# An encoder layer on one core: row scale applied after the projection, head norms ahead of weights, and decayed HGRN keys on GpSimd

## The chip, the cores and the metric

The kernel runs on one core of one Trainium2 chip. The metric is the device time of one execution in microseconds; the median of three runs stands for the kernel. One of the executions is profiled, and all durations below come from that one. Engines are called by the profile's names: PE (TensorE), DVE (VectorE), ACT (ScalarE), POOL (GpSimd) and SP (SyncE, which issues most transfers).

## The reference, cut to what matters

```python
xn = rmsnorm(h, norm_mix[l])            # h: 16 meta tokens and 256 tokens, 2048 wide
proj = xn @ w_in[l]                     # 2048 x 5120
q, f_logit, i_in, g_out, u = jnp.split(proj, [D_HG, 2 * D_HG, 3 * D_HG, 4 * D_HG], axis=-1)
o_hg = hgrn2_mixer(q, f_logit, i_in, g_out, lb_all[l], hg_norm[l])   # 8 heads, 128x128 state
o_s5 = s5_mixer(u, ...)                 # 64 groups, diagonal complex scan, GELU, GLU
h = h + jnp.concatenate([o_hg, o_s5], -1) @ w_out[l]
h = h + conv_ffn(rmsnorm(h, norm_ffn[l]), w_ffn_gate[l], w_ffn_up[l], ..., w_ffn_down[l])
return rmsnorm(h[:, N_META:], final_norm)

def rmsnorm(x, g):                      # one scale per token, one gain per channel
    return x * lax.rsqrt(jnp.mean(x * x, axis=-1, keepdims=True) + EPS) * g
```

## The kernel before, in words

Everything lives in SBUF with channels on the 128 partitions and the 272 tokens along the free dimension. A float32 product is made of three float32r products on PE (`mm3`, lines 193 to 195): high part times high part, high weights times low activations, low weights times high activations. So every operand is split into a high part (a cast on ACT) and a low part (a subtraction). `wload` brings 1 MB of weights into `raw`, `wsplit` makes `whi` on ACT (line 169) and `wlo` on DVE (recorded under the helper `tt`, line 92). There are three buffers of `raw` and three halves of `whi` and `wlo`.

The program begins with a head (lines 220 to 347). It loads x in four pieces, forms for each token the sum of squares and from it the row scale (`row_rs`, `sqrt_rs`), spreads the row scales of the 272 tokens over all partitions with small matmuls into `rbs`, transposes x into `xT`, and for each of 16 channel blocks makes `xn = xT * gm * rbs` on DVE (line 339; `gm` is the gain column times -0.5, which undoes a factor that the row scale carries), `xh` on ACT (line 340) and `xl` on DVE (line 341). The weights of the first chunk are split in quarters, six of the eight `wlo` on POOL. Ten small matmuls (line 312) run on PE ahead of the first product.

Then come 20 chunks of the input projection in the order of `ORDER`: u0, h0, u1, h1, and so on to g3. A `u` is one chunk of S5 channels, an `h` three chunks for two HGRN heads (f, q, i), a `g` one chunk of output gates. One chunk is 96 matmuls of 272 or 258 columns into two PSUM banks. Between the chunk matmuls PE runs the small float32 matmuls of the mixers. `s5_tile` projects (`bu`), scans on DVE with one addition on POOL (`m`, line 605) and projects back (`yps`). `hg_group` forms the scores of two heads level by level: blocks of 4 tokens first (`dps`, with one reciprocal of the running products `SP` over all 512 columns, line 726), then for half lengths 4, 8, 16, 32 and 64 the decayed queries `qh` and keys `kt` (DVE, lines 738 and 740), a matmul `lps` on them, a masked copy into `S`, and `widen`, which multiplies the running products in `SP` and `f` (tile name `PP`) in place. `hg_cross` joins the two token blocks and writes `oT`.

After the chunks, `w_glu` (four units) works on the S5 output, and after unit 1 the head norm `hr` (from `hps` by three Newton steps on DVE) is spread per head by the matmuls `bps`, and `oT`, multiplied by gate and norm, is split into `mh` and `ml`. These are the operands of `w_out`. Then follow the gated MLP and the final norm, which are not touched.

The order of each engine's queue is fixed when the program is built: a scheduler takes the instruction with the lowest priority number that its own estimate says is ready. `pri(x)` shifts that number. Each engine runs its queue in order, and an instruction that waits holds up everything behind it.

Of the kernel before, what the change touches and what calls it, by code (L numbers as in the profile page):

```python
# [80 lines left out]
def hymba_kernel(ctx: ExitStack, tc: tile.TileContext, x, meta, lb_logits, norm_mix, w_in, hg_norm,  # L81
# [76 lines left out]
    def wsplit(raw, eng=(dve, dve), parts=1, dep=None):  # L158
        res = []
        n = 1024 // parts  # L160
        for hf in range(2):
# [2 lines left out]
            if dep is not None and dep[hf] is not None:

                act.copy(out=hi[:, 0:1], in_=dep[hf])
            for i in range(parts):
                c = slice(i * n, (i + 1) * n)
                act.copy(out=hi[:, c], in_=raw[:, hf, c])  # L169
                tt(lo[:, c], raw[:, hf, c], hi[:, c].bitcast(F32), SUB, eng[max(hf, i)])  # L170
# [129 lines left out]
    rm = row_rs(xm, NM, 1, "rm")  # L300
    rb = [None, None]
    for b in range(2):
        rb[b] = row_rs(xt[b], 128, 2, f"rb{b}")
        if b == 0:
            spread(rm, NM, rbp[0][:, 0:NM])
            spread(rb[0], 128, rbp[0][:, NM:])
            act.copy(out=rbs[:, 0:NM + 128], in_=rbp[0])
        else:
            spread(rb[1], 128, rbp[1][:, 0:128])
            dve.tensor_copy(out=rbs[:, NM + 128:T], in_=rbp[1][:, 0:128])  # L310
            for _ in range(NWARM2):
                pe.matmul(wps, ident, rbs[:, NM + 128:T], start=True, stop=True)
# [10 lines left out]
        if b == 0:  # L323
# [4 lines left out]
            gm = prm.tile([128, KD], F32, name="gm")  # L328
            gps = ptp.tile([128, KD], F32, tag="tp", name="gps")
            pe.transpose(gps, nrow, ident[0:KD, 0:KD])  # L330
            ts(gm, gps, -0.5, MUL)
# [468 lines left out]
    def do_u(c):  # L800
# [6 lines left out]
        if c == 1:  # L807
            c_kinds(1)
# [319 lines left out]
```

## Time and profile before

| what | value |
|---|---|
| median of 3 runs | 1227.13 us (1224.62 to 1233.77) |
| the profiled execution | 1229.55 us, its span 1227.8 us |
| PE busy | 1205.0 us, 98% of the span |
| DVE busy | 892.9 us, 73% |
| ACT busy | 623.6 us, 51% |
| POOL busy | 83.2 us, 7% |
| granted TensorE clock, mean | 0.993 |

The span is the time from the first to the last instruction of that execution; 1.75 us lie around it. A share is an average over stages: the 20 chunks end near 355 us, and from there to the end the engines other than PE have much less to do. Matmuls overlap, so that PE counts as busy from the start of one to the modelled end of the next; how far it is from its peak is seen from the distance between starts.

### The profile page before, as it was taken

Reading aid. Unit: us, or ns where it says so; the run is one execution under the profiler, and the core shown is the slowest. Engines: PE = TensorE matmul, PEld = TensorE weight load, DVE = VectorE, ACT = ScalarE, POOL = GpSimd, SP = SyncE. Lnnn points to the kernel's source line nnn. Section 1 sums busy time; section 2 is a strip of 40 time slices with the busy share of each in tenths; the row PEclk is TensorE's granted clock in tenths of the full one; section 3 lists DMA queues with packets and bytes.
Section 4 is the critical chain, followed back from the end, with each engine's and each line's share of the span. In section 5 each row is a group of like instructions: output and inputs, shape, how many; then the busy total and the mean of one; then the engine's idle time right before and its main releaser. Section 6 shows DMA issues by size and latency. Waiting matters only on the chain.

```text
span 1227.8 us, 21177 instructions
## 1 busy us (share of the span) xinstructions
PE 1205.0 (98%) x8531; PEld 1108.1 (90%) x8531; DVE 892.9 (73%) x1516; ACT 623.6 (51%) x1066; POOL 83.2 (7%) x102
## 2 busy tenths in 40 slices
PE   7989999999999999999999999999999999999997
PEld 6989999999989999999999999999999788888885
DVE  8988999999979778766666666765766555555554
ACT  6756667675655466444444444444443344444444
POOL 5231222111100000000000000000000000000000
PEclk9999999999999999999999999999999999999998
DMA  8544344434445555555655556565555545555552
GB/s 255 153 127 143 116 139 128 127 109 138 146 135 175 185 185 172 189 189 177 198 174 190 188 180 194 175 195 182 181 196 172 206 172 204 179 199 199 181 213 93
DMA packets 176289, 210.66 MB, mean 172 GB/s; under 512 B 14772, under 2 KB 168879, under 8 KB 170415
## 3 DMA queue, kind: packets, MB, share of 16 engines
q1 hardware_dynamic: 175871, 209.22, 52.4%
q8 instruction: 67, 1.10, 0.4%
q14 instruction: 31, 0.25, 0.1%
q0 software_dynamic: 320, 0.09, 0.0%
HBM read 206.08 MB, written 2.10 MB: 170 GB/s over the span
## 4 chain that ended last, share of the span: by engine, by line
PE 95%; DVE 2%; issue 1%; DMA 1%; ACT 1%; SPq 0%; POOL 0%; DVEq 0%; ACTq 0%; POOLq 0%
PE ua L976 13%; PE acc L193 10%; PE acc L194 9%; PE acc L195 9%; PE ga L193 7%; PE ga L195 7%; PE ga L194 7%; PE ua L982 7%; PE d L1047 7%; PE d L1049 7%; PE d L1048 7%; PE bu L623 1%; PE lps L753 1%; DVE xn L101 1%; DMA x<-in_x 0%
## 5 line engine op out<-in xcount | busy, mean ns | idle before, releaser
L92 DVE TENSOR_TENSOR wlo<-raw,whi 128x1024 fp32r<-128x1024 f32 (+1 forms) x376 | 462.0, 1229 | 288.6 <-ACT whi L169 238.7
L169 ACT CAST whi<-raw 128x1024 fp32r<-128x1024 f32 (+1 forms) x382 | 397.7, 1042 | 483.1 <-PE ga L194 157.4
L193 PE MATMUL ga<-fh,whi 128*128 128x258 f32 x704 | 198.9, 283 | 0.0
L195 PE MATMUL ga<-fh,wlo 128*128 128x258 f32 x704 | 198.1, 282 | 0.0
L194 PE MATMUL ga<-fl,whi 128*128 128x258 f32 x704 | 198.1, 282 | 0.0
L193 PE MATMUL acc<-xh,whi 128*128 128x272 f32 (+1 forms) x640 | 185.0, 293 | 3.1 <-ACT whi L169 3.1
L194 PE MATMUL acc<-xl,whi 128*128 128x272 f32 (+1 forms) x640 | 185.3, 291 | 1.9 <-DVE xl L92 1.9
L195 PE MATMUL acc<-xh,wlo 128*128 128x272 f32 (+1 forms) x640 | 183.2, 292 | 0.0
L194 PEld LDWEIGHTS ga<-fl,whi 128*128 128x128 f32 x704 | 133.6, 190 | 0.0
L193 PEld LDWEIGHTS ga<-fh,whi 128*128 128x128 f32 x704 | 133.1, 189 | 0.0
L195 PEld LDWEIGHTS ga<-fh,wlo 128*128 128x128 f32 x704 | 132.5, 189 | 0.0
L1048 PE MATMUL d<-whi,al 128*128 128x512 f32 x328 | 128.1, 391 | 0.0
L1047 PE MATMUL d<-whi,ah 128*128 128x512 f32 x328 | 127.4, 393 | 0.3 <-ACT ah L1040 0.3
L193 PEld LDWEIGHTS acc<-xh,whi 128*128 128x128 f32 x640 | 120.1, 189 | 7.1 <-ACT whi L169 3.3
L194 PEld LDWEIGHTS acc<-xl,whi 128*128 128x128 f32 x640 | 120.8, 189 | 4.7 <-DVE xl L92 2.8
L195 PEld LDWEIGHTS acc<-xh,wlo 128*128 128x128 f32 x640 | 119.6, 189 | 2.4 <-issue 1.0
L1049 PE MATMUL d<-wlo,ah 128*128 128x512 f32 x328 | 114.4, 390 | 0.0
L976 PE MATMUL ua<-fcxh,whi 128*128 128x512 f32 x352 | 96.6, 395 | 0.0
L976 PE MATMUL ua<-fcxl,whi 128*128 128x512 f32 x352 | 96.1, 394 | 0.0
L1047 PEld LDWEIGHTS d<-whi,ah 128*128 128x128 f32 x328 | 61.9, 189 | 13.3 <-ACT ah L1040 0.5
L1048 PEld LDWEIGHTS d<-whi,al 128*128 128x128 f32 x328 | 62.0, 189 | 12.9
L1049 PEld LDWEIGHTS d<-wlo,ah 128*128 128x128 f32 x328 | 61.9, 189 | 13.0
(417 smaller groups left out, 1897.7 us busy)
## 6 DMA issues: line engine op xcount, KB each, us to landing
raw<-in_w_ffn_gate SPq DMA_DIRECT2D x44, 1024.0 KB, 5.1
raw<-in_w_ffn_up SPq DMA_DIRECT2D x44, 1024.0 KB, 5.1
raw<-in_w_ffn_down SPq DMA_DIRECT2D x44, 1024.0 KB, 4.8
raw<-in_w_in SPq DMA_DIRECT2D x39, 1024.0 KB, 5.1
raw<-in_w_out SPq DMA_DIRECT2D x16, 1024.0 KB, 5.4
raw<-in_w_glu SPq DMA_DIRECT2D x4, 1024.0 KB, 4.9
x<-in_x SPq DMA_DIRECT2D x4, 512.0 KB, 5.6
out<-ob SPq DMA_DIRECT2D x8, 256.0 KB, 2.9
```

The costliest lines, as they stand in the source:

```text
L92: eng.tensor_tensor(out=dst, in0=a, in1=b, op=op)
L101: dve.scalar_tensor_tensor(out=dst, in0=a, scalar=s, in1=b, op0=op0, op1=op1, **kw)
L169: act.copy(out=hi[:, c], in_=raw[:, hf, c])
L193: pe.matmul(accs[m], lh, xh[:, n0:n1], start=first, stop=False)
L194: pe.matmul(accs[m], lh, xl[:, n0:n1], start=False, stop=False)
L195: pe.matmul(accs[m], ll, xh[:, n0:n1], start=False, stop=end)
L623: return pe.matmul(bus[i][:, ri], bt[h, 2 * ri + q0 // 2], R[h, q0 // 2], start=True, stop=True)
L976: pe.matmul(accs[m].rearrange("p a n -> p (a n)"), hi[:, k * 256 + m * 128:k * 256 + m * 128 + 128], c.rearrange("p a n -> p (a n)"), star ...
L982: pe.matmul(accs[m][:, 0], lo[:, k * 256 + m * 128:k * 256 + m * 128 + 128], c[:, 0], start=False, stop=(kt == KD - 1), skip_group_check=True)
L1047: pe.matmul(dps[t][n], ah[:, tk], hi, start=False, stop=False, skip_group_check=True)
L1048: pe.matmul(dps[t][n], al[:, tk], hi, start=False, stop=False, skip_group_check=True)
L1049: pe.matmul(dps[t][n], ah[:, tk], lo, start=False, stop=end, skip_group_check=True)
```

## The change

It takes the row scale out of the head. `xh` and `xl` are now the split of `xT * gm`, made by an ACT activation with a per-partition scale and one DVE operation, and `xn` and the ten small matmuls are gone. The row scales go to `rcol` (one column per token block) and, spread by three matmuls behind the first chunk, to `rbs`. Every consumer of a projection multiplies by them: `s5_u`, `hg_f`, `hg_q` and `hg_g` with a DVE `tt` from PSUM, `hg_i` by the scale of ACT copies that were there. The eight quarter splits of the first chunk's weights are chained on ACT by `issue_after`, and all eight `wlo` are on DVE. The S5 sum is written into the first half of `P`, whose layout is turned, and the tile `m` goes. The block of 4 tokens takes one reciprocal of 128 columns and builds the other three columns by products. The five larger keys go to POOL. `c_kinds(1)` moves behind the evacuation of u2, and the head norm chain gets `pri(-3)` inside its `pri(-2)`.

```diff
     def wunit(src):
         with pri(-4):
-            return wsplit(early.pop(0), (dve, pool), 2, deps.pop(0)) if early else wsplit(wload(src))
+            return units.pop(0) if units else wsplit(wload(src))
...
-    rm = row_rs(xm, NM, 1, "rm")
-    rb = [None, None]
+    gm = prm.tile([128, KD], F32, name="gm")
+    gps = ptp.tile([128, KD], F32, tag="tp", name="gps")
+    pe.transpose(gps, nrow, ident[0:KD, 0:KD])
+    dve.tensor_copy(out=gm, in_=gps)
...
-            for _ in range(NWARM2):
-                pe.matmul(wps, ident, rbs[:, NM + 128:T], start=True, stop=True)
...
+        def split():
+            i = act.copy(out=hi[:, c], in_=raw)
+            tt(lo[:, c], raw, hi[:, c].bitcast(F32), SUB)
+            return i.ins
+
+        if last is None:
+            wi = split()
+        else:
+            with tc.issue_after(last):
+                wi = split()
+        with tc.issue_after(wi):
+            for kt in (2 * p, 2 * p + 1):
+                last = act.activation(out=xh[:, kt], in_=xT[:, kt], func=AF.Identity, scale=gm[:, kt:kt + 1]).ins
+                stt(xl[:, kt], xT[:, kt], gm[:, kt:kt + 1], xh[:, kt].bitcast(F32), MUL, SUB)
+
+    rcol = s5p.tile([128, 3], F32, name="rcol")
+    rb = [row_rs(xt[0], 128, 2, "rb0")]
+    with pri(0.5):
+        rb += [row_rs(xt[1], 128, 2, "rb1"), row_rs(xm, NM, 1, "rm")]
+    for i, n in enumerate((128, 128, NM)):
+        ts(rcol[:n, i:i + 1], rb[i], -0.5, MUL)
...
-    for kt in range(KD):
-        xn = xin.tile([128, T], F32, tag="xn", name="xn", bufs=4)
-        stt(xn, xT[:, kt], gm[:, kt:kt + 1], rbs, MUL, MUL)
-        act.copy(out=xh[:, kt, :], in_=xn)
-        tt(xl[:, kt, :], xn, xh[:, kt, :].bitcast(F32), SUB)
...
-        act.copy(out=ysb[:, j], in_=pv)
+        tt(ysb[:, j], pv, rv, MUL)
...
-        m = s5w.tile([128, 2, 2 * TH], F32, tag="m", name="m", bufs=1)
-        tt(m, P[:, :, 0], P[:, :, 1], ADD, pool)
+        m = P[:, 0]
+        tt(m, m, P[:, 1], ADD, pool)
...
         for m in range(2):
+            tt(f[:, m], accs[m], rbs, MUL)
+        fact(k, f, AF.Sigmoid, scale=-1.0)
+        fact(f, f, AF.Sigmoid)
...
-            fact(sg[:, m], accs[m], AF.Sigmoid)
-            stt(q[:, m], accs[m], lbc[:, 1, h0 + m:h0 + m + 1], sg[:, m], MUL, MUL)
+            tt(q[:, m], accs[m], rbs[:, T0:T], MUL)
+        fact(sg, q, AF.Sigmoid)
+        for m in range(2):
+            stt(q[:, m], q[:, m], lbc[:, 1, h0 + m:h0 + m + 1], sg[:, m], MUL, MUL)
...
+        tt(r4[:, :, :, 0], s4[:, :, :, 0], f4[:, :, :, 3], MUL)
+        dve.reciprocal(out=r4[:, :, :, 0], in_=r4[:, :, :, 0])
+        tt(r4[:, :, :, 1], r4[:, :, :, 0], s4[:, :, :, 0], MUL)
+        tt(r4[:, :, :, 2], r4[:, :, :, 1], f4[:, :, :, 2], MUL)
+        tt(r4[:, :, :, 0:3], r4[:, :, :, 0:3], q4[:, :, :, 0:3], MUL)
+        act.copy(out=r4[:, :, :, 3], in_=q4[:, :, :, 3])
         widen(2)
         kt = kts[0]
-        dve.reciprocal(out=rv, in_=SP[:, :, NM:T])
         tt(kt.rearrange("p (m b) t -> p m (b t)", b=2), k[:, :, NM:T], SP[:, :, NM:T], MUL)
-        tt(qt, q[:, :, 2:NQ], rv, MUL)
...
             tt(halves(kt.rearrange("p (m b) t -> p m (b t)", b=2), h)[:, :, :, 0],
-               halves(k, h)[:, :, :, 0], halves(SP, h)[:, :, :, 0], MUL)
+               halves(k, h)[:, :, :, 0], halves(SP, h)[:, :, :, 0], MUL, pool)
...
+        if c == 0:
+            rbp = pmm.tile([128, T], F32, tag="mm", name="rbp")
+            spread(rcol[0:NM, 2:3], NM, rbp[:, 0:NM])
+            for b in range(2):
+                spread(rcol[:, b:b + 1], 128, rbp[:, NM + 128 * b:NM + 128 * (b + 1)])
+            act.copy(out=rbs, in_=rbp)
...
-        hrs = rsqrt(hgp, hps, [128, NQ], 1.0 / 128, "rh", tags=("iv", "qm", "v"))
+        with pri(-3):
+            hrs = rsqrt(hgp, hps, [128, NQ], 1.0 / 128, "rh", tags=("iv", "qm", "v"))
```

The change moves instructions on every engine. Three places matter below. The first is DVE in the head, from the last pieces of x to the first operands of the first chunk (`junk` is the discarded square, `rb1`, `rm` the row scales of the second token block and of the meta tokens). Before:

```order
L92 TENSOR_TENSOR wlo<-raw,whi 128x512
L101 SCALAR_TENSOR_TENSOR rb1y<-rb1t,rb1y 128x1
L322 COPY xT<-xps 128x4x128 x2
L310 COPY rbs<-rbp_155 128x128
L96 TENSOR_SCALAR gm<-gps 128x16
L101 SCALAR_TENSOR_TENSOR xn<-xT,gm,rbs 128x272 x4
L92 TENSOR_TENSOR xl<-xn,xh 128x272 x3
```

With the change:

```order
L100 SCALAR_TENSOR_TENSOR junk_139,rb1ss<-x_107 128x512
L95 TENSOR_SCALAR rcol<-rb0y 128x1
L305 COPY xT<-xps 128x4x128
L100 SCALAR_TENSOR_TENSOR junk_139,rmss<-xm 16x1024
L275 TENSOR_REDUCE rb1st<-rb1ss 128x1
L305 COPY xT<-xps 128x4x128
L275 TENSOR_REDUCE rmst<-rmss 16x1
L97 TENSOR_SCALAR rb1v<-rb1st 128x1
L91 TENSOR_TENSOR wlo<-raw,whi 128x512
L97 TENSOR_SCALAR rmv<-rmst 16x1
L100 SCALAR_TENSOR_TENSOR xl<-xT,gm,xh 128x272 x2
```

The first `xl` no longer stands behind the spreading of the row scales and four `xn`, but the square of the meta tokens now stands between the two last `xT` copies.

The second place is DVE in the levels of the first HGRN group, where `qh` is the decayed query and the two `widen` products are those on `SP` and `PP`; what an instruction waits for is in brackets:

```order
L91 TENSOR_TENSOR qh<-q,PP 128x256 [waits DVE_49]
L91 TENSOR_TENSOR SP<-SP,PP 128x34x8 [waits Pool_49]
L100 SCALAR_TENSOR_TENSOR pt<-pw 128x32 [waits DVE_49]
L100 SCALAR_TENSOR_TENSOR pw<-pw 128x32
L100 SCALAR_TENSOR_TENSOR W<-W,pw,tmp 128x2x34 [waits Activation_49] x2
L91 TENSOR_TENSOR PP<-PP 128x34x8 [waits DVE_49]
L91 TENSOR_TENSOR km<-k,SP 128x2x16
L95 TENSOR_SCALAR pw<-pt 128x32 [waits DVE_49]
L91 TENSOR_TENSOR wlo<-raw,whi 128x1024 [waits PE_49,Activation_49]
L91 TENSOR_TENSOR qh<-q,PP 128x256 [waits DVE_49]
```

The key that stood next to each `qh` has left DVE, and the in-place product on `SP` now waits until POOL has read `SP` for its key.

The third place is PE where `w_glu` ends and `w_out` begins. Before, the first spread of the head norm stands inside the third and fourth unit of `w_glu` (`gh` are the S5 operands):

```order
L194 MATMUL acc<-gh_4662,whi 128x258
L893 MATMUL bps<-hr,hsel 128x258 x2
L195 MATMUL acc<-gh_4662,wlo 128x258
L193 MATMUL acc<-gh_4663,whi 128x258
L194 MATMUL acc<-gh_4663,whi 128x258
```

With the change it stands behind the last one, right ahead of the first products that need `mh`:

```order
L188 MATMUL acc<-gh_4632,wlo 128x258
L918 MATMUL bps<-hr,hsel 128x258 x4
L186 MATMUL acc<-mh,whi 128x258 x3
L918 MATMUL bps<-hr,hsel 128x258 x2
L187 MATMUL acc<-ml,whi 128x258
L188 MATMUL acc<-mh,wlo 128x258
```

The first four `bps` have moved from between products of `w_glu` to the seam between the two matrices.

More of the change, by code (lines that the diff above doesn't have):

```diff
@@ L163, in wsplit @@
             lo = wsp.tile([128, 1024], F32R, tag="wlo", name="wlo")
[L164 to L170, printed above, removed]
+            act.copy(out=hi, in_=raw[:, hf])
+            tt(lo, raw[:, hf], hi.bitcast(F32), SUB)
             res.append((hi, lo))
@@ L234, in hymba_kernel @@
     sp.dma_start(out=xm, in_=meta)
+    sp.dma_start(out=nrow, in_=norm_mix.rearrange("o (r c) -> (o r) c", c=128))
     HD = D // 2
@@ L292, in hymba_kernel @@
         pe.matmul(wps, ident, ident, start=True, stop=True)
-    rbp = [pmm.tile([128, NM + 128], F32, tag="mm", name=f"rbp{b}") for b in range(2)]
-    rbs = xin.tile([128, T], F32, name="rbs")
+    rbs = s5p.tile([128, T], F32, name="rbs")
     def spread(r, n, ps):
         pe.matmul(ps, r.to_broadcast([n, 128]), ident[0:n, 0:n], start=True, stop=True)
-    rm = row_rs(xm, NM, 1, "rm")
-    rb = [None, None]
+    gm = prm.tile([128, KD], F32, name="gm")
+    gps = ptp.tile([128, KD], F32, tag="tp", name="gps")
+    pe.transpose(gps, nrow, ident[0:KD, 0:KD])
+    dve.tensor_copy(out=gm, in_=gps)
     for b in range(2):
[L303 to L310, printed above, removed]
-            for _ in range(NWARM2):
-                pe.matmul(wps, ident, rbs[:, NM + 128:T], start=True, stop=True)
         for i in range(4):
@@ L327, in hymba_kernel @@
             act.copy(out=xT[:, :, 0:NM], in_=xps)
[L328 to L331, printed above, removed]
+    last = None
+    for p in range(8):
+        u, hf, c = p // 4, p // 2 % 2, slice(512 * (p % 2), 512 * (p % 2) + 512)
+        if p % 4 == 0:
+            units.append([])
+        if p % 2 == 0:
+            units[u].append([wsp.tile([128, 1024], F32R, tag=t, name=t) for t in ("whi", "wlo")])
+        hi, lo = units[u][hf]
+        raw = early[u][:, hf, c]
+        def split():
[17 more added lines that the diff above has]
+        ts(rcol[:n, i:i + 1], rb[i], -0.5, MUL)
     tc.cur_priority += 900000
     pool.memset(ones, 1.0)
-    tc.cur_priority -= 900000
-    for kt in range(KD):
-        xn = xin.tile([128, T], F32, tag="xn", name="xn", bufs=4)
-        stt(xn, xT[:, kt], gm[:, kt:kt + 1], rbs, MUL, MUL)
-        act.copy(out=xh[:, kt, :], in_=xn)
-        tt(xl[:, kt, :], xn, xh[:, kt, :].bitcast(F32), SUB)
-    tc.cur_priority += 900000
-    deps[:] = [(None, xh[:, 0, 0:1].bitcast(F32)), tuple(xh[:, i, 0:1].bitcast(F32) for i in (3, 6))]
     vps = ptp.tile([128, 100], F32, tag="tp", name="vps")
@@ L568, in s5_u @@
     def s5_u(j, ps):
-        pv = ps.rearrange("p (k s) -> p s k", s=2)
-        act.copy(out=ysb[:, j], in_=pv)
+        pv, rv = (a.rearrange("p (k s) -> p s k", s=2) for a in (ps, rbs))
+        tt(ysb[:, j], pv, rv, MUL)
     def s5_split(j):
@@ L801, in do_u @@
         accs = chunk(w_in, 16 + c)
+        if c == 0:
+            rbp = pmm.tile([128, T], F32, tag="mm", name="rbp")
+            spread(rcol[0:NM, 2:3], NM, rbp[:, 0:NM])
+            for b in range(2):
+                spread(rcol[:, b:b + 1], 128, rbp[:, NM + 128 * b:NM + 128 * (b + 1)])
+            act.copy(out=rbs, in_=rbp)
         with pri(-3):
@@ L804, in do_u @@
                 s5_u(2 * c + m, accs[m])
+        if c == 2:
+            c_kinds(1)
         for m in range(2):
             s5_tile(2 * c + m, *s5_split(2 * c + m), *s5_b(2 * c + m))
[L807 to L808 removed]
     def do_h(g):
```

41 lines of the change are left out of this document (20 added, 21 removed).

## The prediction

> **What bounds the kernel now.** I read the busy shares first (busy us, share of the span, instructions of each engine).
>
> ```profile
> PE 1205.0 (98%) x8531; PEld 1108.1 (90%) x8531; DVE 892.9 (73%) x1516; ACT 623.6 (51%) x1066; POOL 83.2 (7%) x102
> ```
>
> PE sets the end, but the shares average over stages, so the table of stretches comes next (us; busy time and instructions of PE, PEld, DVE, ACT and POOL; granted clock; DMA share; GB/s).
>
> ```profile
> 17.00:20.40 3.40, 3.40 (x19) 3.40 (x19) 3.40 (x7) 2.78 (x8) 1.58 (x2) 0.54 1.13 332
> 20.00:100.00 80.00, 73.35 (x591) 70.66 (x591) 72.03 (x202) 49.39 (x101) 25.82 (x34) 0.98 0.51 150
> 85.20:88.60 3.40, 3.40 (x18) 3.40 (x18) 3.40 (x6) 0.87 (x2) 2.91 (x4) 0.53 1.03 340
> 100.00:300.00 200.00, 199.98 (x1789) 186.38 (x1789) 197.35 (x349) 133.41 (x331) 37.03 (x41) 1.00 0.41 126
> 300.00:355.00 55.00, 55.00 (x489) 49.94 (x488) 47.87 (x82) 30.30 (x68) 6.81 (x3) 1.00 0.44 139
> ```
>
> From 100 us on PE is full, and DVE nearly: 197.35 of 200 us. Whatever is gained must come from before 100, and DVE has 2.65 us of room in the 200 that follow. What is lost before 100 stands in the list of PE's waits (total us, times, longest), and the head in the timeline (start, duration, idle before in brackets).
>
> ```profile
> PE acc L193 <- ACT whi L169: 3.1, 1, 3.1
> PE acc L194 <- DVE xl L92: 1.9, 2, 1.8
> PE ktp L560 <- ACT bt L556: 1.0, 1, 1.0
> PE cps L520 <- ACT ccx L89: 0.4, 1, 0.4
> PE btp L555 <- ACT eb L552: 0.2, 1, 0.2
> ```
>
> ```profile
> 4.21 1.21 DVE L101 SCALAR_TENSOR_TENSOR junk<-xm 16x1024 bf16<-16x1024 f32 x1 [3.10 <-DMA xm<-in_meta_tokens]
> 11.05 0.68 DVE L101 SCALAR_TENSOR_TENSOR junk<-x 128x512 bf16<-128x512 f32 x1
> 12.11 0.68 DVE L322 COPY xT<-xps 128x512 f32<-128x512 f32 x1
> 13.03 0.68 DVE L92 TENSOR_TENSOR wlo<-raw,whi 128x512 fp32r<-128x512 f32 x1
> 16.31 4.12 PE L312 MATMUL wps<-rbs,ident 128*128 128x128 f32 x20 [0.31 <-DVE rbs L310]
> 16.45 1.74 DVE L101 SCALAR_TENSOR_TENSOR xn<-xT,gm,rbs 128x272 f32<-128x272 f32 x4
> 20.19 0.49 PE L193 MATMUL acc<-xh,whi 128*128 128x272 f32 x2
> ```
>
> The first product starts at 20.19, behind the spread row scales, four `xn` and the ten small matmuls. These rows hold all that can be won: 20.19 us of head, of which the arrival of x stays, and waits of 6.6 us. The later stages are full.
>
> **Start of the products.** Without `xn` DVE needs, from the last square of x (11.05, plus 0.43 us because another transfer goes ahead of x), 0.68 for it, 0.68 and 0.68 for two `xT` copies, 1.21 for the meta square that moved between them, about 0.9 for seven small operations and 0.68 for `wlo`: 16.3 us. PE starts on `xh` and `whi`, ready slightly earlier: 16.2, so 4.0 us sooner (2.5 to 4.6). From there a quarter of the chunk takes DVE half a `wlo` of 1.23 us (row at 373.58 below) and two `xl`, 0.43 each by the key below with 272 for 256 columns: 1.5 us, what twelve products at 0.12 us take. So the two `xl` waits of 1.9 us should vanish. Against them PE gets three spreads. Ten small ones took 4.12 us at half clock, 0.2 each at full; with the evacuation around them I take 0.7 (0.5 to 1.2). **Terms: -4.0 and -1.2** (the second -1.9 to +0.5).
>
> **The clock.** In 17.00 to 20.40 the granted clock was 0.54, and again in 85.20 to 88.60, behind the wait of 3.1 us. The ten small matmuls took the first of these slow stretches. Now products take it: 3.4 us at half speed lose at most 1.7, less where the operands limit anyway. I take **+1.2** (0 to 1.7).
>
> The Trainium skill speaks against dropping these matmuls: "TensorE: Matmul & The Clock Gate", Part 1, says that about 3.4 us of idling halves PE's clock, and that about 3.4 us of work restore it, however many matmuls that is. By that rule the term would be the full 1.7 and the time half a microsecond longer; the trace agrees in the length of both stretches.
>
> **The waits of 40 to 84.** In the changed queue some 30 products stand between `btp` and `ktp`, so the 1.0 and 0.2 should go. The 3.1 us has its history on POOL.
>
> ```profile
> 73.08 6.76 POOL L92 TENSOR_TENSOR bt<-br,abr 128x64 f32<-128x64 f32 x1 [12.62 <-DMA br<-in_s_b_re]
> 79.81 0.29 POOL L92 TENSOR_TENSOR bt<-br,xi 128x64 f32<-128x64 f32 x1
> 81.18 0.94 ACT L552 COPY eb<-br 64x256 f32<-64x256 f32 x2 [7.05 <-POOL br L92]
> 83.36 0.39 PE L193 MATMUL acc<-xh,whi 128*128 128x272 f32 x1 [3.06 <-ACT whi L169]
> ```
>
> One `bt` that normally takes 0.29 took 6.76, while DVE ran two-input operations without a break; ACT waited 7.05 for `eb`, and the weight cast queued behind it came late. The change moves `c_kinds(1)`, not this `bt`, and lays the neighbourhood differently. I count half of 3.1, and half of the slow clock behind it (0.8). **Term: -3.6** (0 to -6.2: all waits and 1.7 of clock).
>
> **DVE and GpSimd in the groups.** The rows for the sum (count | busy, mean ns | idle before), and what one engine does to the other:
>
> ```profile
> L726 DVE RECIPROCAL rv<-SP 128x512 f32<-128x512 f32 x4 | 13.4, 3340 | 0.0
> L815 DVE RECIPROCAL f<-PP 128x2 f32<-128x2 f32 x4 | 0.6, 155 | 0.0
> L92 DVE TENSOR_TENSOR qt<-q,rv 128x512 f32<-128x512 f32 x4 | 2.9, 717 | 0.0
> L92 DVE TENSOR_TENSOR kt<-k,SP 128x256 f32<-128x256 f32 x20 | 8.2, 411 | 0.0
> L101 DVE SCALAR_TENSOR_TENSOR q<-acc,lbc,sg 128x258 f32<-128x258 f32 x8 | 3.8, 473 | 0.0
> L101 DVE SCALAR_TENSOR_TENSOR xn<-xT,gm,rbs 128x272 f32<-128x272 f32 x16 | 10.4, 687 | 0.1
> L92 POOL TENSOR_TENSOR m<-P 128x544 f32<-128x544 f32 x16 | 28.5, 1779 | 166.1 <-DVE P L92 166.1
> L101 DVE SCALAR_TENSOR_TENSOR W<-W,pw,tmp 128x34 f32<-128x34 f32 x32 | 10.3, 357 | 0.0
> L92 DVE TENSOR_TENSOR P<-W,m 128x1088 f32<-128x1088 f32 x16 | 20.6, 1285 | 0.0
> ```
>
> ```profile
> 107.96 1.62 DVE L101 SCALAR_TENSOR_TENSOR W<-W,pw,tmp 128x34 f32<-128x34 f32 x2
> 108.12 1.41 POOL L92 TENSOR_TENSOR m<-P 128x544 f32<-128x544 f32 x1 [20.00 <-DVE P L92]
> 156.66 0.41 DVE L92 TENSOR_TENSOR kt<-k,SP 128x256 f32<-128x256 f32 x1
> 158.96 1.00 PE L753 MATMUL lps<-qh,kt 128*128 128x64 f32 x8
> ```
>
> Removed: four reciprocals of 3.34 and four `qt` of 0.72 (16.2 us), twenty keys (8.2). Added: a reciprocal of 128 columns, between 0.155 at 2 and 3.34 at 512, by proportion 0.95; three products of 128 columns at about 0.30 and one of 384 at 0.55: 2.4 a group, 9.6 in all. Six scalings of 0.47 for `f`, `q` and `u` in each of four pairs: 11.3. A key on POOL lies between 0.29 (`bt`, 64 columns) and 1.41 (`m`, 544): 0.74 by proportion. While POOL ran `m` for 1.41 us, two `W` took 1.62 instead of 0.71, so DVE lost 0.9 us, 0.65 of POOL's time; twenty keys at that rate lose it 9.6. So moving the keys frees nothing on DVE, and the groups hold +6.1 us more in all. The room is the 2.65 us above, 7.1 in 300 to 355, and what DVE gains ahead of chunk 1, where `xn` drops out (10.4, much of it stretched beside POOL).
>
> For a key itself the cover is the stretch from its end (157.07) to the `lps` (158.96), 1.9 us; 0.33 more for the key and a hand-over fit. The in-place product on `SP` now waits for POOL with other DVE work ahead of it, 20 times; if the cover is gone, 0.33 each makes 6.6. What is queued behind it on DVE is `wlo`, on which PE waits next. I take **+1.5** for all this, 0 to 12 (the worst is rival C), nearer to 0 because the sixteen `m` took 1.78 on the average against 1.41 undisturbed, beside a DVE as full as it will be.
>
> **The seam ahead of `w_out`.**
>
> ```profile
> 371.70 0.40 PE L893 MATMUL bps<-hr,hsel 128*128 128x258 f32 x2
> 372.39 0.75 DVE L92 TENSOR_TENSOR oT<-oT,bps 128x258 f32<-128x258 f32 x2
> 373.58 1.23 DVE L92 TENSOR_TENSOR wlo<-raw,whi 128x1024 fp32r<-128x1024 f32 x1 [0.44 <-ACT whi L169]
> 374.13 0.70 ACT L895 CAST mh<-oT 128x258 fp32r<-128x258 f32 x2
> 375.40 0.76 DVE L92 TENSOR_TENSOR ml<-oT,mh 128x258 fp32r<-128x258 f32 x2
> ```
>
> Now `bps` stand in PE's own queue right ahead of the product that needs `mh`. From 371.70 to the end of the two `ml` it took 4.46 us; a single one needs 0.20, 0.38, 0.35 and 0.38, 1.3 us, and a `wlo` in its way 1.23 more. PE fills 1.2 us with `bps` and three products that it had anyway. So a new wait of 0.7 to 4: I take **+2.0**.
>
> **Sum.** -4.0 -1.2 +1.2 -3.6 +1.5 +2.0 = -4.1. The profiled span of 1227.8 becomes 1223.7; that execution was 1.75 us longer than its span, and its 1229.55 lies 2.4 above the median, so I put the change on the median: 1223.0.
>
> **Rivals.** *A: the sum as above*, 0.45. *B: every wait before 84 goes and nothing is paid back*: -4.0 -1.9 +0.7 -4.7 -1.7 +1.2, with the seam at 0.7: -9.7, 1217.4. For it speaks that each wait had a single cause; against it that DVE is as full as before. 0.17. *C, the other side: keys starve on GpSimd* as the `bt` at 73.08 did, behind an unbroken row of two-input DVE work. A starved key arrives 6.76 - 0.41 = 6.35 us later, 1.9 of that is cover, so PE loses 4.4 each time; with one the gain of 4.1 is gone, from two on it is a loss, and with four (less the 1.5 counted) the time is 1227.1 - 4.1 + 16.1 = 1239. For it: that row, and DVE at 197 of 200; against it: the sixteen `m`, at 1.78 on the average. 0.13.
>
> On C the Trainium skill, "SBUF — State Buffer", section "Who interferes with whom", says that GpSimd and a DVE instruction with two SBUF inputs exclude each other for one whole instruction, the first to issue winning. By that alone a key would wait for one DVE operation, at most 1.29 us, and C could not be; the 6.76 us do not agree, so I leave C its chance.
>
> *D: DVE becomes the bound*: the +6.1 in the groups outrun the 2.65, and what PE gained before 100 is waited away on `wlo`, so that `w_glu` starts where it did; with the seam 1229. For it the full DVE, against it the room before 100 and behind 300. 0.2. *E: the first products wait as now*, because the weights or x, not DVE's chain, bound the start (the DMA share was 1.13 in 17.00 to 20.40): neither the 4.0 nor the 1.2 of the first chunk comes, 1228. Against it, x was squared at 11.05 and the weights cast before 13.03. 0.05.
>
> **Chances and range.** A measurement of this kernel tells about 1% from no change, that is below 1214.9 or above 1239.4. The best ends of all terms make -12.0, 1215.1, so faster needs B and a little more than the rows bound: 0.08. Slower needs C with four or more keys, or D with the bad ends: 0.09. The rest, 0.83. The worst ends make +15.7, 1243; the range that leaves out C's far end is 1215 to 1237.
>
> **What would show it.** First product near 16.2; no `xl` wait of over 0.5 us in the first chunk; granted clock near 0.5 for some 3.4 us from there; chunk ends about 5 to 9 us earlier at 100; keys on POOL at 0.7 to 0.8; a PE wait of some 2 us ahead of the first `mh` product. I am wrong if the first product comes after 18, if PE waits between 100 and 300 add up to over 3 us (C or D: on `kt` or on `wlo`), or if the seam costs over 4.

## The result and the profile after

The changed kernel takes 1234.62 us in the median of 20 runs (1233.35 to 1238.84), the kernel before 1226.81 us in as many (1223.04 to 1233.77): a ratio of 1.0062, interval 1.0049 to 1.0076. The change makes it slower by some 7.8 us. The time lies inside the predicted range, but on the other side of the time before than forecast: 1223.0 had been put as likeliest. That it still lies inside is owed to the width of the range, not to the mechanism.

The profiled execution took 1236.91 us, its span 1235.1, so 7.3 us more than the span before. The page's first part and the table of stretches, which answer to those of before:

```profile
PE 1208.3 (98%) x8511; PEld 1110.1 (90%) x8511; DVE 886.9 (72%) x1532; ACT 624.4 (51%) x1051; POOL 102.9 (8%) x116
```

```profile
20.00:100.00 80.00, 79.64 (x661) 78.55 (x660) 71.51 (x216) 54.99 (x107) 18.19 (x27) 0.98 0.57 169
85.20:88.60 3.40, 3.40 (x30) 3.40 (x30) 2.53 (x6) 1.48 (x3) 3.40 (x7) 1.00 0.25 65
100.00:110.00 10.00, 7.60 (x56) 6.47 (x54) 10.00 (x18) 4.58 (x13) 5.46 (x3) 1.00 0.49 158
110.00:120.00 10.00, 7.21 (x51) 5.90 (x52) 9.08 (x21) 4.31 (x14) 3.21 (x2) 0.74 0.00 1
120.00:130.00 10.00, 10.00 (x89) 9.29 (x87) 9.74 (x19) 8.73 (x21) 1.40 (x1) 0.75 0.24 76
100.00:300.00 200.00, 193.60 (x1718) 177.41 (x1717) 195.28 (x355) 130.46 (x327) 61.10 (x55) 0.97 0.37 114
300.00:355.00 55.00, 53.67 (x468) 51.36 (x467) 43.52 (x76) 26.28 (x47) 11.45 (x5) 1.00 0.47 151
```

Between 20 and 100 us PE now idles next to nothing (79.64 of 80 busy, against 73.35), and the slow clock at 85 is gone. The loss has moved behind 100: 5.2 us of idling in 100 to 120, and a clock of 0.74 and 0.75 in 110 to 130, which is 10.2 us at half speed. From 100 to 355 PE idles for 7.7 us in all, where before it idled for 0.02. DVE as a whole is busy for 6.0 us less than before.

Where the time went is best seen from PE's starts at equal places in the program: the first product, the start of the seventh and of the eighth chunk (chunks 6 and 7, counted from 0), the start of `w_glu`, and the product 96 places into `w_out`. A stretch is the difference of two starts.

| stretch on PE | before, us | after, us | difference |
|---|---|---|---|
| up to the first product | 20.2 | 15.2 | -5.0 |
| chunk 0 | 16.2 | 17.2 | +0.9 |
| chunks 1 to 5 | 78.5 | 70.6 | -7.8 |
| chunk 6 | 15.1 | 30.3 | +15.2 |
| chunk 7 to `w_glu` | 224.9 | 221.8 | -3.1 |
| `w_glu` to 96 products into `w_out` | 36.3 | 45.1 | +8.8 |
| the rest | 836.6 | 835.0 | -1.7 |

At the start of chunk 6 the changed kernel leads by 11.9 us (102.95 against 114.87). At the start of `w_glu` nothing is left (355.02 against 354.87), and the seam behind it takes 9 us more. The rest is the same work in both. Its -1.7 is a half clock of 3.4 us at 979 in the profile before, behind a wait of PE for `us` of 1.8 us that both kernels have; all five profiles with the old head show it, and two of the thirteen with the new one. So the 1.7 us are a matter of the clock, and no run shows whether the change has a part in them.

The list of PE's waits (total us, times, longest; the lines that bear on this) names DVE where it named the casts and `xl`:

```profile
PE lps L766 <- DVE S L774: 2.6, 2, 2.3
PE mps L800 <- DVE qm L91: 1.8, 1, 1.8
PE lps L771 <- DVE S L774: 1.6, 2, 1.3
PE acc L187 <- DVE xl L100: 1.1, 1, 1.1
PE bps L918 <- DVE oT L91: 0.7, 2, 0.4
PE acc L186 <- ACT mh L920: 0.6, 1, 0.6
```

`S` is the masked copy of an HGRN level, `qm` the operand of the join behind the levels: in chunk 6 PE waits for the levels of the first HGRN group, and at the seam for the head norm.

**The last HGRN group in the timeline of DVE.** First before, then after (start, duration). `PP` in line 95 or 96 finishes the forget gates `f`, `SP<-SP,PP` is `widen(2)`, `S<-masks,dps` is the first level:

```profile
259.32 0.41 DVE L96 TENSOR_SCALAR PP<-PP 128x544 f32<-128x544 f32 x1
264.79 0.43 DVE L92 TENSOR_TENSOR SP<-SP,PP 128x272 f32<-128x272 f32 x1
267.08 3.34 DVE L726 RECIPROCAL rv<-SP 128x512 f32<-128x512 f32 x1
275.43 0.47 DVE L101 SCALAR_TENSOR_TENSOR q<-acc,lbc,sg 128x258 f32<-128x258 f32 x1
278.16 0.47 DVE L101 SCALAR_TENSOR_TENSOR q<-acc,lbc,sg 128x258 f32<-128x258 f32 x1
286.18 0.73 DVE L733 COPY_PREDICATED S<-masks,dps 128x512 f32<-128x512 int32 x1
```

```profile
266.79 1.19 DVE L95 TENSOR_SCALAR PP<-PP 128x544 f32<-128x544 f32 x1
282.06 0.86 DVE L100 SCALAR_TENSOR_TENSOR q<-q,lbc,sg 128x258 f32<-128x258 f32 x2
284.44 0.39 DVE L91 TENSOR_TENSOR qt<-SP,PP 128x128 f32<-128x128 f32 x1
286.06 0.95 DVE L739 RECIPROCAL qt<-qt 128x128 f32<-128x128 f32 x1
289.66 1.56 DVE L91 TENSOR_TENSOR qt<-qt,SP 128x128 f32<-128x128 f32 x1
292.99 0.44 DVE L91 TENSOR_TENSOR SP<-SP,PP 128x272 f32<-128x272 f32 x1
294.94 1.04 DVE L91 TENSOR_TENSOR qt<-qt,q 128x384 f32<-128x384 f32 x1
302.87 0.74 DVE L751 COPY_PREDICATED S<-masks,dps 128x512 f32<-128x512 int32 x1
```

Before, the reciprocal starts 7.8 us behind the gates, ahead of `q`, which comes from the group's next chunk. After, the gates come 7.5 us later, and the reciprocal starts 19.3 us behind them and only when `q` is done. Its columns lie in the buffer of `sg`, the sigmoid of `q`, which must be read first (`qt = hgp.tile([128, 2, 256], F32, tag="sg", name="qt")`; before, `rv` had the buffer "qm", and only the later product with `q` went into "sg"). And `widen(2)`, which overwrites `SP` and `PP` in place, stands behind the chain, at 292.99 instead of 264.79. The reciprocal itself is shorter, and the level arrives later: it is copied at 302.87 instead of 286.18. Before, the long reciprocal was over when `q` came, and the level followed 7.6 us behind `q` (278.63 to 286.18); now the whole chain lies between them, and it takes 20.0 us (282.92 to 302.87).

**The seam** in the timeline of PE, behind the DVE rows that finish `hr`, before and after:

```profile
368.73 0.48 DVE L101 SCALAR_TENSOR_TENSOR hr<-rhy,misc,ht 128x258 fp32r<-128x258 f32 x1
378.64 0.48 DVE L100 SCALAR_TENSOR_TENSOR hr<-rhy,misc,ht 128x258 fp32r<-128x258 f32 x1
```

```profile
381.17 0.40 PE L918 MATMUL bps<-hr,hsel 128*128 128x258 f32 x2
381.97 0.72 PE L918 MATMUL bps<-hr,hsel 128*128 128x258 f32 x2 [0.40 <-DVE oT L91]
383.33 0.63 PE L186 MATMUL acc<-mh,whi 128*128 128x258 f32 x3 [0.64 <-ACT mh L920]
384.62 0.58 PE L918 MATMUL bps<-hr,hsel 128*128 128x258 f32 x1 [0.28 <-DVE oT L91]
```

`hr` is ready at 379.1, some 10 us later than before (369.2), PE reaches the products of `w_out` with pauses of 0.3 to 0.6 us each, and ten of the sixteen small matmuls of `hps`, all of which lay ahead of `w_glu`, now cost their 3 us inside it (its first 96 products take 14.6 instead of 11.6 us).

### The profile page after: what moved, and what is told of

The parts are those of the page before. It is cut to its first block, busy times and chain, and to the rows that moved or that the text cites. A ratio compares the mean times of both kernels' runs of the same rounds, so it can differ in the third digit from the quotient of the medians.

```text
span 1235.1 us, 21186 instructions
## 1 busy us (share of the span) xinstructions
PE 1208.3 (98%) x8511; PEld 1110.1 (90%) x8511; DVE 886.9 (72%) x1532; ACT 624.4 (51%) x1051; POOL 102.9 (8%) x116
## 4 chain that ended last, share of the span: by engine, by line
PE 84%; DVE 9%; issue 2%; POOL 1%; DMA 1%; ACT 1%; SPq 0%; DVEq 0%; POOLq 0%; ACTq 0%
PE ua L1001 13%; PE acc L187 7%; PE acc L186 7%; PE acc L188 7%; PE ga L186 7%; PE ga L188 7%; PE ga L187 7%; PE ua L1007 7%; PE d L1072 6%; PE d L1074 6%; PE d L1073 6%; DVE wlo L91 2%; DVE P L91 2%; DVE W L100 1%; POOL P L91 1%
## 5 line engine op out<-in xcount | busy, mean ns | idle before, releaser
L162 ACT CAST whi<-raw 128x1024 fp32r<-128x1024 f32 x374 | 392.7, 1051 | 453.2 <-PE ga L187 157.6
L187 PE MATMUL acc<-xl,whi 128*128 128x272 f32 (+1 forms) x640 | 188.3, 295 | 1.1 <-DVE xl L100 1.1
L186 PE MATMUL acc<-xh,whi 128*128 128x272 f32 (+1 forms) x640 | 187.5, 296 | 1.4 <-ACT xh L335 0.7
L188 PE MATMUL acc<-xh,wlo 128*128 128x272 f32 (+1 forms) x640 | 187.1, 295 | 0.0
L186 PEld LDWEIGHTS acc<-xh,whi 128*128 128x128 f32 x640 | 122.6, 192 | 4.2 <-DVE PP L91 1.2
L187 PEld LDWEIGHTS acc<-xl,whi 128*128 128x128 f32 x640 | 123.4, 193 | 2.9 <-DVE xl L100 1.3
L188 PEld LDWEIGHTS acc<-xh,wlo 128*128 128x128 f32 x640 | 122.6, 193 | 2.5 <-issue 1.0
L187 PE MATMUL acc<-ml,whi 128*128 128x258 f32 x256 | 73.1, 288 | 0.1
```

The costliest lines, as they stand in the source:

```text
L162: act.copy(out=hi, in_=raw[:, hf])
L186: pe.matmul(accs[m], lh, xh[:, n0:n1], start=first, stop=False)
L187: pe.matmul(accs[m], lh, xl[:, n0:n1], start=False, stop=False)
L188: pe.matmul(accs[m], ll, xh[:, n0:n1], start=False, stop=end)
```

## The experiments

Each was timed beside the kernel before on the same chip; ratios are to that, with their intervals. The changed kernel's own is 1.0062 (1.0049 to 1.0076), and run once more beside the later ones:

**The changed kernel again** (after_again).

> The changed kernel itself once more, beside the other one on the same chip: 1233 to 1236, and a first chunk whose length differs by up to 3 us from the 17.2 us of the first profile if the slow clock at its start varies from run to run.

1233.24 us, ratio 1.0063 (1.0050 to 1.0075). Its stretches: first product 14.2, chunk 0 17.0, chunk 6 29.0, `w_glu` at 354.8, the seam stretch 42.6. The loss in chunk 6 repeats; of the seam, 2.5 us do not, as is seen below. Chunk 0 hardly differs between these two; it does against the profile of a_fullrecip, below.

**Keys back on DVE** (a_keysdve), and **only the keys moved, in the kernel before** (b_keyspool):

```diff
-               halves(k, h)[:, :, :, 0], halves(SP, h)[:, :, :, 0], MUL, pool)
+               halves(k, h)[:, :, :, 0], halves(SP, h)[:, :, :, 0], MUL)
```

> The changed kernel with the twenty larger HGRN keys back on DVE. Theory (from about 100 us on DVE is the bound, and the lead of the early start is waited away on it): DVE gets 20 x 0.41 = 8 us of keys back but loses no time to GpSimd's reads beside it, so 1232 to 1237, no change against 1234.6. Rival (the keys on GpSimd, 2 us each in the changed profile, hold up the levels): 1225 to 1229, and the PE waits of 103 to 120 us vanish.

> The kernel before with only the twenty larger keys moved to GpSimd. Theory (DVE's total is what counts, the move is nearly neutral for it): 1226 to 1229. Rival (keys on GpSimd hold up the levels): 1231 or more, with PE waits on lps behind 100 us.

a_keysdve: 1236.70 us, ratio 1.0093 (1.0080 to 1.0106), inside the theory's bracket, but by the intervals not the time of the change: the keys on POOL help the changed kernel by some 2 to 4 us. b_keyspool: 1231.32 us, ratio 1.0048 (1.0036 to 1.0061): they hurt the kernel before by 4.9. The second is what the rival expected, but not for its reason. The group of keys on POOL in the changed kernel (count | busy, mean ns | idle before):

```profile
L91 POOL TENSOR_TENSOR kt<-k,SP 128x256 f32<-128x256 f32 x20 | 29.4, 1471 | 53.3 <-DVE SP L91 48.3 <-PE lps L771 4.4 <-DVE pt L100 0.6
```

A key takes 1.47 us, twice the estimate, and yet the levels run no slower: from the first to the fourth masked copy of a group it is 17.0, 20.6, 19.7 and 19.7 us after, 17.2, 20.6, 19.6 and 21.1 before. In b_keyspool no PE wait on `lps` is over 0.3 us. The longest key of the changed kernel took 3.06 us, against the 6.76 of rival C. What costs the 4.9 us in b_keyspool is not seen in PE's waits and stays open.

**Twelve small matmuls behind the second product** (a_late), meant to take the lead away:

```diff
+    for _ in range(12):
+        pe.matmul(wps, ident, xT[:, KD - 1, NM + 128:T], start=True, stop=True)
```

> The changed kernel with twelve small matmuls behind its second product, so that the chunks begin some 5 us later, as late as before, at full clock. Theory (DVE is the bound behind 100 us): the lead is worth nothing, 1232 to 1236, and PE's waits of 100 to 120 shrink by what the start lost. Rival (the lead is real and the loss comes from elsewhere): 1237 to 1240.

1238.61 us, ratio 1.0102 (1.0088 to 1.0115). The test failed as such: chunk 0 still ended at 32.4, since the first product came 0.9 us earlier and the half clock at the start lasted 3.4 us instead of 6.8. The kernel lost elsewhere (`w_glu` at 358.8), and the run decides nothing between the theories.

**Without the row scale in the consumers** of u, f, q and g (a_noscale), which the computation then lacks:

```diff
-        tt(ysb[:, j], pv, rv, MUL)
+        act.copy(out=ysb[:, j], in_=pv)
...
-            tt(f[:, m], accs[m], rbs, MUL)
...
```

> The changed kernel without the row scale in the consumers of u, f, q and g (left out of the computation: the row scale is only in the values v), so that DVE has 32 operations of about 0.45 us less and ACT copies u as before. Theory (DVE is the bound): 14 us less on DVE bring the HGRN end and the spread of the head norm back inside w_glu, 1220 to 1228. Rival (keys on GpSimd): within 2 us of 1234.6.

1228.64 us, ratio 1.0027 (1.0014 to 1.0039). Six microseconds come back, but `w_glu` starts at 355.5 as ever; what is saved is at the seam (36.4 us, as before). The time is just above the theory's bracket: the scalings do matter, and `hr` comes at 369.8 without them, as before the change, though the last group's first level is as late as 297.0.

**The last HGRN group ahead of the last S5 chunk** (a_order): `ORDER = "u0 h0 u1 h1 u2 h2 h3 u3 g0 g1 g2 g3"`.

> The changed kernel with h3 ahead of u3 in the order of the chunks, so that the last HGRN group and the head norm end some two chunks sooner and the spreads bps lie inside w_glu again. Theory (the seam ahead of w_out costs about 5.8 us, 2.8 of waits and 3 of slow clock, and the rest of the loss lies at 103 to 126): 1227 to 1230. Rival (DVE paces all of it, so lateness only changes its place): 1232 to 1236.

1239.21 us, ratio 1.0092 (1.0060 to 1.0123). The seam stretch falls to 35.7 us, and the stretch from chunk 7 to `w_glu` grows to 235.0. The rival is right in kind, and 3 us too low: bringing HGRN forward alone only moves the lateness, now to S5, whose last split ends at 361.8 instead of 333.7.

**The reciprocal over 512 columns in the changed kernel** (a_fullrecip), **the same with the keys back too** (a_headonly):

```diff
-        tt(r4[:, :, :, 0], s4[:, :, :, 0], f4[:, :, :, 3], MUL)
-        dve.reciprocal(out=r4[:, :, :, 0], in_=r4[:, :, :, 0])
...
         widen(2)
+        rv = hgp.tile([128, 2, 256], F32, tag="qm", name="rv")
+        dve.reciprocal(out=rv, in_=SP[:, :, NM:T])
...
+        tt(qt, q[:, :, 2:NQ], rv, MUL)
```

> The changed kernel with the reciprocal of SP over 512 columns as before, 6.6 us more on DVE by the prediction's terms, and an order in which the last HGRN group stands earlier. Theory (what DVE gains in the groups and what the seam costs are about alike): 1231 to 1237. Rival (only the load on DVE counts): 1239 to 1243.

> The changed kernel with the reciprocal and the keys as before, so that only the head, the scalings, the place of c_kinds and the layout of P are changed. Theory (head and scalings are what costs, reciprocal and keys help a little): 1236 to 1242. Rival (the head alone gains, the mixers' parts lose): 1221 to 1228.

a_fullrecip: 1227.31 us, ratio 1.0008 (0.9990 to 1.0027), no different from before and 7 us faster than the change, below what was expected. a_headonly: 1238.17 us, ratio 1.0087 (1.0056 to 1.0119), as expected: DVE carries all the keys and the scalings, `w_glu` starts at 342.8, and then PE waits 4.1 us for `hr` at one place. So the worth of the one edit hangs on the other: with the keys on POOL, the long reciprocal gains 7 us (a_fullrecip against the changed kernel), with the keys on DVE less than 1 (1.0087 against the 1.0093 of a_keysdve, no difference by the intervals); and with the long reciprocal the keys on POOL gain 11. The same group on DVE in a_fullrecip:

```profile
256.56 0.43 DVE L95 TENSOR_SCALAR PP<-PP 128x544 f32<-128x544 f32 x1
260.22 0.44 DVE L91 TENSOR_TENSOR SP<-SP,PP 128x272 f32<-128x272 f32 x1
262.13 3.34 DVE L740 RECIPROCAL rv<-SP 128x512 f32<-128x512 f32 x1
274.69 0.86 DVE L100 SCALAR_TENSOR_TENSOR q<-q,lbc,sg 128x258 f32<-128x258 f32 x2
284.39 0.74 DVE L748 COPY_PREDICATED S<-masks,dps 128x512 f32<-128x512 int32 x1
```

`widen(2)` and the reciprocal stand right behind the gates again, ahead of `q`, and the first level is copied at 284.39.

**The one reciprocal alone, in the kernel before** (b_recip): the lines taken out above, put into it.

> The kernel before with only the one reciprocal of 128 columns and its products, ahead of widen(2) as in the change; by the prediction's terms 6.6 us less on DVE. Theory now (the chain ahead of the in-place widen(2) delays each group's first level, S5 work takes its room on DVE, and the HGRN end and the head norm come late): 1230 to 1235, first level of the last group 8 us or more later than at 286.2, bps at the seam. Rival (DVE's load decides): 1219 to 1225.

1232.07 us, ratio 1.0046 (1.0031 to 1.0062), as the theory of the delayed chain had it, against the load: this edit alone costs the kernel before 6 us. Its first level of the last group is copied at 298.2. How DVE fares at the end shows in the stretch from 300 to 363.2 us, where the changed kernel's last `hps` runs: before, after, a_fullrecip, b_recip.

```profile
300.00:363.20 63.20, 63.20 (x557) 58.14 (x556) 55.23 (x96) 34.74 (x74) 6.81 (x3) 1.00 0.43 137
```

```profile
300.00:363.20 63.20, 61.87 (x524) 57.62 (x522) 49.05 (x86) 30.47 (x54) 11.45 (x5) 1.00 0.45 148
```

```profile
300.00:363.20 63.20, 61.94 (x541) 57.02 (x541) 57.97 (x103) 36.14 (x74) 4.55 (x4) 1.00 0.42 138
```

```profile
300.00:363.20 63.20, 62.52 (x524) 57.75 (x524) 45.19 (x81) 29.00 (x53) 4.73 (x1) 1.00 0.46 150
```

With the one reciprocal DVE idles 14 and 18 us there, with the long one 8 and 5. The S5 work has gone ahead: the last S5 split ends at 349.5 before and 353.0 in a_fullrecip, at 333.7 after and 327.5 in b_recip. What is left for the end is HGRN's tail, one step waiting for the next.

**What it is in the one reciprocal.** Four kernels take single features of it: `widen(2)` ahead of the reciprocal, with two ACT copies of the columns that it overwrites (a_unchain); the reciprocal's columns in the buffer that `rv` had, not in that of `sg`, in the changed kernel (a_ownbuf) and in b_recip (b_recip_own); and the kernel before with nothing but the buffers of `rv` and `qt` exchanged (b_sgbuf):

```diff
-        qt, rv = (hgp.tile([128, 2, 256], F32, tag=t_, name=n_) for t_, n_ in (("sg", "qt"), ("qm", "rv")))
+        qt, rv = (hgp.tile([128, 2, 256], F32, tag=t_, name=n_) for t_, n_ in (("qm", "qt"), ("sg", "rv")))
```

> The changed kernel with widen(2) ahead of the reciprocal: ACT first copies the two columns that widen(2) overwrites, and the product SP x f falls away, since widen(2) makes it. Theory: the first levels come 3 to 8 us sooner than in the change, 1226 to 1231. Rival (the number of dependent steps, not their place ahead of widen(2), holds up the group): 1233 to 1236.

> The changed kernel with the columns of the reciprocal in a buffer of their own (the one that rv had before), and only the last product, by q, in the buffer that the sigmoid sg of q had; the same operations. Theory (in the change the whole chain, and widen(2) behind it, waits until q has let go of sg): the reciprocals of the later groups start within 10 us behind f instead of 15 to 20, the last group's first level comes 10 us or more sooner than at 302.9, 1223 to 1228. Rival (the six dependent steps hold up the group): 1231 to 1235.

> The kernel before with the one reciprocal of 128 columns, its columns in rv's buffer. Theory (the buffer is what costs): 1222 to 1228, against 1232 with the shared buffer. Rival (the steps cost): 1230 to 1233.

> The kernel before, with nothing changed but that rv and qt exchange their buffers, so that the reciprocal over 512 columns waits until q has let go of sg; no operation added or taken away. Theory: the reciprocals start behind q, the HGRN end comes some 5 us later, 1229 to 1234. Rival (buffers do not matter): 1225 to 1227.

In this order: 1232.69 us, ratio 1.0055 (1.0041 to 1.0069); 1232.76 us, 1.0049 (1.0031 to 1.0068); 1235.84 us, 1.0074 (1.0053 to 1.0095); 1229.08 us, 1.0017 (1.0000 to 1.0035). Neither feature alone is the cause: the theory fell in the first three (the rival's bracket held only in a_ownbuf), and in the fourth the time lies at the lower edge of the theory's bracket. In a_ownbuf the reciprocals of the later groups do start 7 to 10 us behind the gates, as expected, and the time is nearly that of the change. In b_sgbuf the reciprocals do start behind `q`; the time is about 2 us longer, by an interval that begins at no difference. b_recip_own even lost 5.2 us in one wait of PE on a copy of `i`, which no theory here foresaw.

**Both together** (a_both; of the lines taken out, only the last is shown):

```diff
...
+        cf = hgp.tile([128, 2, 2, 64], F32, tag="qh", name="cf", bufs=3)
+        act.copy(out=cf[:, 0], in_=s4[:, :, :, 0])
+        act.copy(out=cf[:, 1], in_=f4[:, :, :, 2])
+        widen(2)
+        r3 = hgp.tile([128, 2, 64, 3], F32, tag="qm", name="rr")
+        dve.reciprocal(out=r3[:, :, :, 0], in_=s4[:, :, :, 0])
+        tt(r3[:, :, :, 1], r3[:, :, :, 0], cf[:, 0], MUL)
+        tt(r3[:, :, :, 2], r3[:, :, :, 1], cf[:, 1], MUL)
+        tt(r4[:, :, :, 0:3], r3, q4[:, :, :, 0:3], MUL)
...
-        widen(2)
```

> The changed kernel with both: widen(2) ahead of the reciprocal (two ACT copies keep the columns it overwrites), and the reciprocal's columns in a buffer that does not wait for q. Theory (the two waits hide each other, so that taking away either alone brought only some 2 us): 1225 to 1229. Rival (neither decides; the added dependent steps and the order that the planner makes of them do): 1231 to 1234.

1229.41 us, ratio 1.0030 (1.0019 to 1.0041), 3.8 us less than the changed kernel beside it and just above the expected bracket. The seam stretch is 38.4 us, `hr` comes at 370.0 and `w_glu` at 352.7, near the 369.2 and 354.9 before the change. In the last group:

```profile
264.15 0.80 DVE L95 TENSOR_SCALAR PP<-PP 128x544 f32<-128x544 f32 x1 [0.30 <-ACT PP L88]
270.64 0.43 DVE L91 TENSOR_TENSOR SP<-SP,PP 128x272 f32<-128x272 f32 x1
273.24 0.94 DVE L743 RECIPROCAL rr<-SP 128x128 f32<-128x128 f32 x1
293.66 0.72 DVE L754 COPY_PREDICATED S<-masks,dps 128x512 f32<-128x512 int32 x1
```

The reciprocal is back at 9.1 us behind the gates, but the first level comes at 293.66, 9.3 us later than in a_fullrecip with its more than three times longer reciprocal.

**One reciprocal over three columns** (a_recip3), 384 columns into the buffer of `sg`, behind `widen(2)`:

> The changed kernel with one reciprocal over the three columns of a block that are not 1 (384 columns, about 2.5 us) behind widen(2), so 4 us less on DVE in all than with 512 columns. Theory (place of the chain and DVE's load): 1223 to 1228. Rival (where the planner puts the last group decides: it puts the head norm's matmuls as late as in the change): 1231 to 1236.

1230.75 us, ratio 1.0043 (1.0026 to 1.0060): between the two brackets. Less work on DVE than in a_fullrecip, and slower.

**Filling the seam** (a_seamfill):

```diff
                 tt(oT[:, h], oT[:, h], bp, MUL)
+                if h < 4:
+                    wp = psc.tile([128, 256], F32, tag="sc", name="wp")
+                    pe.matmul(wp, ident, oT[:, h, 0:256], start=True, stop=True)
```

> The changed kernel with one small matmul of 256 columns behind each of the first four products oT x bps, so that PE idles less at the seam ahead of w_out. Theory (about 3 us of the seam are the slow clock that follows the idling): 1231 to 1233.5, and no window of half clock behind the seam. Rival (the seam costs only its waits): 1235 to 1237, since the added matmuls cost up to 0.4 us each.

1233.76 us, ratio 1.0056 (1.0038 to 1.0074); the clock at the seam stayed at 1.00 and the stretch was 42.8 us instead of 45.1. But the changed kernel's second profile, without these matmuls, has full clock there too and 42.6 us. The run cannot tell whether the filling kept the clock up; the time lies between the two brackets and is that of the change.

## Why the prediction was wrong

**The head was right, and more.** The first `xl` was reckoned from the rows at 16.3 us:

```profile
16.23 0.89 DVE L100 SCALAR_TENSOR_TENSOR xl<-xT,gm,xh 128x272 fp32r<-128x272 f32 x2
```

The first product came at 15.17, a microsecond ahead of the forecast, and the second waited 1.1 for that `xl`, where no wait of over 0.5 had been expected. The waits of 40 to 84 went altogether: chunks 1 to 5 gained 7.8 where 3.6 was put and 6.2 held for the most. The lead, predicted as 5 to 9 at 100 us, was 11.9 at the start of chunk 6.

**The clock in the head was a term with a spread, not a size.** The granted clock in 15.00 to 18.40 and 18.40 to 21.80, first after, then a_fullrecip, whose head is the same code:

```profile
15.00:18.40 3.40, 2.15 (x9) 1.93 (x10) 3.40 (x10) 3.40 (x9) 2.45 (x6) 0.61 1.09 347
18.40:21.80 3.40, 3.40 (x17) 3.40 (x16) 3.40 (x10) 3.40 (x10) 0.00 (x0) 0.50 1.18 310
```

```profile
15.00:18.40 3.40, 2.41 (x19) 2.41 (x20) 3.40 (x9) 3.40 (x9) 1.71 (x5) 1.00 1.09 349
18.40:21.80 3.40, 3.40 (x29) 3.40 (x29) 3.40 (x11) 3.40 (x10) 0.00 (x0) 1.00 1.23 296
```

Chunk 0 took 17.2 us in the one and 14.7 in the other, 2.5 us apart; 0 to 1.7 had been allowed. Over the thirteen profiles with the new head the half clock near the first product lasted 6.8 us in five (chunk 0 took 17.0 to 17.3 us), 3.4 in five (16.0 to 16.1, or 18.1 with the twelve matmuls of a_late), and did not come in three (14.4 to 14.7). The Trainium skill, "TensorE: Matmul & The Clock Gate", Part 1, says that the window by which the clock is set runs freely and does not begin with the kernel, so that the number of slow matmuls varies from run to run. The two profiles agree with that, in more than the half microsecond by which it lets the transition vary.

**The step that failed is the one on DVE and GpSimd in the groups, +1.5.** From the start of chunk 6 to `w_glu`, where the groups lie, the changed kernel lost 12.1 us against the kernel before (+15.2 and -3.1 in the table). That is the whole lead. PE's waits there, 7.7 us, and the half clock that followed two of them, 10.2 us at half speed or some 5.1 lost, cover it; for a half clock in the groups the sum had no term. Of the signs of being wrong that the prediction named, two came true: waits of over 3 us between 100 and 300 (6.4), and a seam of over 4.

The step priced the block reciprocal by its duration, 2.4 us a group instead of 4.1, as a relief. The duration was right: 0.95 for the reciprocal, as estimated, a product of 128 columns 0.39 instead of 0.30; and DVE is busy no longer than before between 60 and 340 us (270.1 against 271.3). What was not asked is when the chain can start and what stands behind it. Its first step writes into the buffer of `sg` and so waits for `q`, and `widen(2)` waits for the chain, with all five levels behind. Both stand in the code.

Shown is what the edit costs: undone in the changed kernel, it gives 7 us back (a_fullrecip), and put alone into the kernel before, it takes 6 (b_recip), at less work. It does not cost this in every surrounding: with the keys on DVE, undoing it gains less than 1 (a_headonly against a_keysdve). Nor is it the only part whose removal helps: without the scalings 6 us come back too (a_noscale). How it costs is shown in part. Taking away both waits gives 3.8 back (a_both); some 3 us to a_fullrecip remain, which is not clear of the noise of the two. That these are due to the number of dependent steps, between which the scheduler lays S5 work, fits the S5 work that ends 16 to 22 us earlier than before in every one of these chains, but no run isolates it: it stays open.

The sum also left out the eight scalings of `g`, 0.42 us each or 3.3 in all, which lie behind 314 us; and the best end of its term for the waits would be -6.4 by its own rows, not -6.2. Neither changes the sign.

The `pri(-3)` around the head norm and the new place of `c_kinds(1)` were not taken away alone; that they have no share is not shown.

**The seam was named and undersized.** +2.0 was put, 0.7 to 4 held; the stretch grew by 6.3 (second profile) and 8.8 (first). Of that 3.0 are the `hps` matmuls, which the sum had left out and which earlier stretches no longer hold; some 3.3 lie around the waits, whose pauses alone are 1.4; 2.5 are slow clock in the one profile and not in the other. The seam is no cause of its own: it is where a late `hr` is paid. In all eighteen profiles the stretch follows how far the end of `hr` lies behind the first product of `w_glu`. Up to 15.3 us behind (14.3 before, 15.3 in a_fullrecip) it takes 35.7 to 36.4 us; 17.2 to 19.8 behind, 38.2 to 39.3; 22.2 to 25.0 behind (24.1 after), 41.7 to 43.3, or 45.0 to 45.7 where 6.8 us of half clock are added; and 38.3 behind (a_headonly), 56.4.

**Of the rivals, D was half right.** It said that `w_glu` would start where it did, and it starts at 355.0 against 354.9. In a_fullrecip the lead is 14.7 us at chunk 6 and 2.9 at `w_glu`, and DVE is busy for 276.5 of the 280 us from 60 to 340:

```profile
60.00:340.00 280.00, 275.70 (x2444) 259.33 (x2442) 271.30 (x484) 176.91 (x425) 56.23 (x56) 0.99 0.43 133
```

```profile
60.00:340.00 280.00, 272.28 (x2411) 253.77 (x2411) 270.11 (x512) 176.69 (x421) 88.66 (x81) 0.98 0.41 126
```

```profile
60.00:340.00 280.00, 272.89 (x2437) 255.16 (x2436) 276.53 (x492) 175.99 (x415) 75.75 (x75) 0.99 0.40 126
```

(Before, after, a_fullrecip.) That fits a head start lost to a DVE that has nothing to spare, but does not show it: in a_noscale DVE idles for 14.4 us of the same 280, and `w_glu` starts no earlier (355.5); in a_headonly it idles for 4.7, and `w_glu` starts 12 us earlier than before. So why undoing the reciprocal only brings the time back to that of before, and not below it, stays open. In the changed kernel itself DVE has 10 us of idling there, so that its total load does not explain why the kernel is slower than before. Rival C fell: the keys are slower than estimated, but PE's longest wait in the levels ended with DVE's masked copy at 109.89, when the key had been ready since 108.49, and in the groups DVE waited for a key once, for 1.3 us.

**The forecast that the time would stay within 1%** came true with a ratio of 1.0062; the forecast sign did not, and a ratio of 1 lies outside the measured interval.

## What to carry to other kernels

A shorter instruction in place of a long one is no gain until three things are checked at its place: which buffer it writes into and who last reads that, which in-place operation must wait for it, and how many dependent steps it has become. And a lead of the engine that sets the end is worth only what is left of it at the end: read that engine's waits and its clock over the whole stretch in which the lead must last, not the lead alone. Where an order is made by a scheduler, try each part of an edit alone in both kernels, and in pairs: the keys on GpSimd were worth -2 to -4 us in the changed kernel, -11 in it with the long reciprocal, and +4.9 in the kernel before.
